# Batched matmul, 32 x (512x1024 by 1024x768): stores 0 to 10 move from the even to the odd turns of the load loop

## The chip, the cores and the metric

The kernel runs on one core of one Trainium2 chip. The metric is device time in microseconds (us), the median of several executions; smaller is better. The core has a matrix engine (TensorE, PE in the profile), three engines for copies and element work (VectorE or DVE, ScalarE or ACT, GpSimd or POOL), a synchronising engine (SyncE or SP), and 16 DMA engines that move data between the device's memory (HBM) and the core's own memory (SBUF). PE writes its results to a small accumulator memory (PSUM). DMAs are issued by an engine's instruction stream and then run from a queue: POOL feeds the software queue q0, SP the hardware queue q1.

## The reference

```python
batch, m, k, n = 32, 512, 1024, 768
x = np.random.randn(batch, m, k).astype(np.float32)
weight = np.random.randn(batch, k, n).astype(np.float32)

def reference(x, weight):
    return np.matmul(x, weight).astype(np.float32)
```

There are 32 independent products. Each reads 2 MiB of x and 3 MiB of weight and writes 1.5 MiB of result, all float32 in HBM. The whole problem reads 167.77 MB and writes 50.33 MB.

## The kernel before

**Tiling.** Two batch entries form a pair, so there are 16 pairs, 0 to 15. The x of a pair is one DMA of 4 MiB on the HBM side, the weights of a pair are one DMA of 6 MiB (called w(k) here for pair k; the first two pairs and the last one are loaded as two DMAs of one entry each), and a finished pair's results are one store of 3 MiB. x and w become bf16 on the way into SBUF. The page of the profile gives the bytes of such a load on the SBUF side, half of those read.

**Buffers.** There are two x slots, two pairs' worth of w slots and four output slots (`W_SLOTS, X_SLOTS, OUT_SLOTS = 4, 2, 4`, the first counted in entries). Output slot a % 4 can be written again when the store of pair a - 4 has landed: `slot_free` (line 231) makes ACT wait for that before its first copy of a pair, and lets DVE go on through the semaphore `s_free`.

**PE** (`on_pe`, from line 192) goes through the pairs in order. For each pair it transposes x in 8 groups (line 174, result tile `pt`, spread by DVE into `xT` at line 220, or 228 for the last pair), and then multiplies: 2 entries x 4 row tiles, each 16 matmuls on lines 139 and 166 into the six accumulator tiles `pm`. It takes a ready signal for the pair's x ahead of the transposes and one for each entry's w ahead of that entry's matmuls.

**ACT and DVE** copy the accumulators into the output slots (lines 262 and 266 on ACT, 271 and 273 on DVE). The copy at line 273 is the last one of half an entry. DVE does the last copy of pair k only after it has spread the transposes of pair k + 1.

**POOL** (`on_pool`) issues nearly all the DMAs, in the program's order, and waits in that order too. The loop is written out for 14 turns, k = 0 to 13. Turn k issues x(k + 2), when the first row tile of pair k has been multiplied (`mm_begun(k)`, line 110); then, in some turns, stores; then w(k + 2), when pair k has been multiplied completely (line 97; the two entries of pair 15 have a wait each, line 101). A store (`store`, line 117) first waits until ACT and DVE have copied the whole pair. Behind the loop POOL issues stores 11, 12 and 13. q0 works these DMAs off in the order of issue.

**SP** waits for each load of w and passes the signal on to PE, and then issues the last output itself: store 14, and the output of pair 15 in four quarters (lines 119 and 124) as its entries' halves are copied.

The diff touches one condition in `on_pool`; the loop counts `PAIRS = 16`, `HELD = 2`.

Of the kernel before, what the change touches and what calls it, by code (L numbers as in the profile page):

```python
# [12 lines left out]
def kernel(  # L13
# [16 lines left out]
    PAIRS = B // 2  # L30
# [62 lines left out]
    def load_w(b):  # L93
        if together(b):
            if b % 2 == 0:
                pool.wait_ge(s_mm, mm_done(b + 1 - W_SLOTS))
                slots = all_ws[:, b // 2 % 2].rearrange("p r ko n -> p r (ko n)")
                pool.dma_start(out=slots, in_=w_two_view[b // 2]).then_inc(s_w[b % W_SLOTS], 16)  # L98
            return
        if b >= W_SLOTS:  # L100
            pool.wait_ge(s_mm, mm_done(b - W_SLOTS))
        pool.dma_start(out=ws[b % W_SLOTS], in_=w_view[b]).then_inc(s_w[b % W_SLOTS], 16)  # L102
# [5 lines left out]
    def load_x(k):  # L108
        if k >= X_SLOTS:
            pool.wait_ge(s_mm, mm_begun(k - X_SLOTS))  # L110
        pool.dma_start(out=xs[k % X_SLOTS], in_=x_view[k]).then_inc(s_x[k % X_SLOTS], 16)  # L111
# [5 lines left out]
    def store(eng, a, sem):  # L117
        copied(eng, 4 * a + 3)
        eng.dma_start(out=two_view[a], in_=outs[a % OUT_SLOTS]).then_inc(sem, 16)  # L119
# [222 lines left out]
    def on_pool():  # L342
        load_w(0)
        pool.memset(ident, 0.0).then_inc(s_zero, 1)  # L344
        pool.wait_ge(s_zero, 1)
        pool.affine_select(  # L346
            out=ident,
            in_=ident,
            compare_op=mybir.AluOpType.not_equal,
            fill=1.0,  # L350
            base=0,
            pattern=[[-1, P]],
            channel_multiplier=1,
        ).then_inc(s_ident, 1)
        load_w(1)
        load_x(1)
        load_w(2)
        load_w(3)
        def stores(first, last):
            for a in range(max(first, 0), last):  # L360
                store(pool, a, s_st[a % OUT_SLOTS])


        for k in range(PAIRS - 2):
            load_x(k + 2)
            if k % 2 == 0:
                stores(k - 3, k - 1)
            load_w(2 * k + 4)
            load_w(2 * k + 5)
        stores(PAIRS - 3 - HELD, PAIRS - 2)  # L370
# [21 lines left out]
    with tc.tile_critical(sync_engine=mybir.EngineType.Activation, no_gpsimd_drain=True):  # L392
        sp.dma_start(x_first, x_view[0]).then_inc(s_first, 16)
        on_pool()
        on_pe()
        on_dve()
        on_act()
        on_sp()
        clear_on_pool()
# [30 lines left out]
```

## Time and profile before

| what | before |
|---|---|
| median of 3 runs | 512.89 us (512.43 to 513.11) |
| span of the profiled execution, first to last instruction | 510.1 us |
| median minus that span (what lies around it) | 2.8 us |
| PE busy | 422.5 us, 83% |
| DVE busy | 212.8 us, 42% |
| ACT busy | 115.8 us, 23% |
| POOL busy | 29.0 us, 6% |
| mean granted PE clock | 0.951 |

The profile is of one execution, and gives no time for it beside the span. A row of a timeline or a group reads: start, duration (or busy time and mean), engine, line of the kernel, operation, tiles, count, and in square brackets the idle time of that engine ahead of it with what ended it. DMA-issuing instructions last about half a microsecond; how long the data takes stands in the DMA views, as the time from the issue to the landing of the last byte. In the rows of time stretches, the number behind PEclk's place is the granted TensorE clock, then come the mean busy share of the 16 DMA engines (it can come out a little over 1, since packets overlap) and the rate, which counts a load by its bf16 bytes.

### The profile page before, as it was taken

The numbers are of one execution on the slowest core, as the hardware profiler recorded it, in microseconds if no ns is written. First come the engines' busy times: TensorE is split into PE (matmuls) and PEld (weight loads), VectorE is DVE, ScalarE is ACT, GpSimd is POOL, SyncE is SP. The second block draws the span as 40 slices with busy tenths as digits, with TensorE's granted clock in tenths as the row PEclk, the third lists the DMA queues.
The fourth block names the chain that finished last, engine by engine and source line by source line (L and its number), as shares of the span: only waits on it lengthen the run. The fifth ranks groups of instructions, "written<-read, shape, count | busy, mean of one in ns | idle before, by whom it ended". The sixth has DMA issues, their size and how long they took to land. (4 is left out here: it accounts for less than half of the span.)

```text
span 510.1 us, 5783 instructions
## 1 busy us (share of the span) xinstructions
PE 422.5 (83%) x2512; PEld 172.3 (34%) x1536; DVE 212.8 (42%) x332; ACT 115.8 (23%) x197; POOL 29.0 (6%) x54
## 2 busy tenths in 40 slices
PE   0199999999999599993999939999499984999990
PEld 0143425353525134251343403434144331343420
DVE  0253636454536136351463513635145441454631
ACT  1313131313231221302313023130222302223130
POOL 2000001000100001000010000100001000100000
PEclk9999999999999899997999969999799995999996
DMA  8999999999999999999999999999999999999997
GB/s 296 261 213 216 217 215 220 212 299 251 214 217 224 432 241 218 215 229 432 233 219 216 244 432 216 220 216 259 419 216 218 219 272 405 215 215 236 434 427 336
DMA packets 9443, 136.34 MB, mean 267 GB/s; under 512 B 864, under 2 KB 864, under 8 KB 1376
## 3 DMA queue, kind: packets, MB, share of 16 engines
q0 software_dynamic: 8576, 125.83, 95.7%
q1 hardware_dynamic: 864, 10.49, 5.0%
q14 instruction: 3, 0.02, 0.0%
HBM read 167.77 MB, written 50.33 MB: 428 GB/s over the span
## 5 line engine op out<-in xcount | busy, mean ns | idle before, releaser
L166 PE MATMUL pm<-w,xT 128*128 x976 | 328.2, 386 | 36.3 <-DVE outs L271 36.3
L139 PE MATMUL pm<-w,xT 128*128 x1024 | 283.9, 277 | 4.7 <-DVE xT L220 1.7
L166 PEld LDWEIGHTS pm<-w,xT 128*128 128x128 bf16 x1024 | 101.8, 99 | 275.4 <-issue 235.8
L271 DVE COPY outs<-pm 64x512 f32<-64x512 f32 x128 | 88.1, 688 | 199.8 <-DVEq L269 198.4
L262 ACT COPY outs<-pm 64x512 f32<-64x512 f32 x128 | 74.1, 579 | 264.1 <-PE pm L139 163.2
L174 PE MATMUL pt<-ident,x 128*128 128x128 f32 x512 | 84.5, 307 | 33.4 <-PEq L178 23.1
L220 DVE COPY xT<-pt 128x1024 bf16<-128x1024 bf16 x120 | 77.8, 687 | 63.4 <-PE pt L174 63.0
L174 PEld LDWEIGHTS pt<-ident,x 128*128 128x128 f32 x512 | 71.2, 210 | 48.7 <-issue 26.5
L266 ACT COPY outs<-pm 64x512 f32<-64x512 f32 x64 | 37.0, 578 | 99.9 <-PE pm L139 99.8
L273 DVE COPY outs<-pm 64x512 f32<-64x512 f32 x64 | 43.9, 685 | 0.0
L98 POOL DMA_DIRECT2D w<-in_weight_dram x13 | 9.2, 706 | 260.0 <-PE pm L139 260.0
L111 POOL DMA_DIRECT2D x<-in_x_dram x15 | 8.3, 555 | 127.3 <-PE pm L139 88.7
L281 DVE CAST x<-outs 128x1024 bf16<-128x1024 f32 x4 | 2.5, 690 | 18.9 <-DMA outs<-in_x_dram 18.9
L119 POOL DMA_DIRECT2D out_dram<-outs x14 | 7.5, 537 | 7.1 <-DVE outs L273 7.1
L281 ACT CAST x<-outs 128x1024 bf16<-128x1024 f32 x4 | 3.9, 1042 | 16.6 <-DMA outs<-in_x_dram 16.6
L228 DVE COPY xT<-pt 128x512 bf16<-128x512 bf16 x16 | 5.7, 418 | 4.1 <-PE pt L174 4.1
L102 POOL DMA_DIRECT2D w<-in_weight_dram x6 | 3.4, 564 | 29.1 <-PE pm L139 27.9
L281 ACT ACT_TABLE_LOAD x1 | 1.3, 1283 | 1.0 <-ACTq L392 1.0
L346 POOL TENSOR_SCALAR_AFFINE_SELECT ident<-ident 128x128 f32<-128x128 f32 x1 | 0.3, 282 | 0.2 <-POOL ident L344 0.2
L344 POOL MEMSET ident<- 128x128 f32 x1 | 0.2, 223 | 0.0
L414 POOL MEMSET const-float32-0.0<- 128x1 f32 x1 | 0.1, 98 | 0.2 <-issue 0.2
L414 POOL MEMSET const-bfloat16-1.0<- 128x1 bf16 x1 | 0.1, 102 | 0.0
(2 smaller groups left out, 0.2 us busy)
## 6 DMA issues: line engine op xcount, KB each, us to landing
out_dram<-outs POOLq DMA_DIRECT2D x14, 3072.0 KB, 39.0
w<-in_weight_dram POOLq DMA_DIRECT2D x13, 3072.0 KB, 29.1
x<-in_x_dram POOLq DMA_DIRECT2D x15, 2048.0 KB, 30.4
w<-in_weight_dram POOLq DMA_DIRECT2D x6, 1536.0 KB, 29.8
outs<-in_x_dram SPq DMA_DIRECT2D x1, 4096.0 KB, 18.0
out_dram<-outs SPq DMA_DIRECT2D x1, 3072.0 KB, 18.8
out_dram<-outs SPq DMA_DIRECT2D x4, 768.0 KB, 15.2
```

The costliest lines, as they stand in the source:

```text
L98: pool.dma_start(out=slots, in_=w_two_view[b // 2]).then_inc(s_w[b % W_SLOTS], 16)
L111: pool.dma_start(out=xs[k % X_SLOTS], in_=x_view[k]).then_inc(s_x[k % X_SLOTS], 16)
L119: eng.dma_start(out=two_view[a], in_=outs[a % OUT_SLOTS]).then_inc(sem, 16)
L139: return pe.add_instruction(mybir.InstMatmult(name=nc.get_next_instruction_name(), engine=mybir.EngineType.PE, ins=[pe.lower_ap(moving), p ...
L166: last = pe.matmul(*args, start=(ko == 0), stop=(ko == KT - 1))
L174: last = pe.transpose(pts[g % 2][:, j, :], words[:, mo, j::JT], ident)
L220: return dve.tensor_copy(both[g // 2][:, :, :, g % 2].rearrange("p b j i r -> p j b i r"), pt)
L262: last = act.copy(*piece)
L266: act.copy(*pieces(b, p, 2)[0]).then_inc(s_ap, 1)
L271: last = dve.tensor_copy(*piece)
L273: dve.tensor_copy(*pieces(b, p, 2)[1]).then_inc(s_dp, 1)
L281: last = copy(xs[0][:, mo], x_first[:, mo])
```

## The change

```diff
         for k in range(PAIRS - 2):
             load_x(k + 2)
-            if k % 2 == 0:
-                stores(k - 3, k - 1)
+            if k % 2 and k < PAIRS - 3:
+                stores(k - 2, k)
             load_w(2 * k + 4)
             load_w(2 * k + 5)
         stores(PAIRS - 3 - HELD, PAIRS - 2)
```

`stores(first, last)` issues stores first to last - 1, leaving out negative numbers. Before, store 0 stands in turn 2, and the couples (1, 2), (3, 4), (5, 6), (7, 8) and (9, 10) in turns 4, 6, 8, 10 and 12, always between that turn's x and its w. After, store 0 stands in turn 1 and the couples in turns 3, 5, 7, 9 and 11; turn 13 has none. So each of these 11 stores is issued one turn earlier, and the younger store of turn k is that of pair k - 1 instead of k - 2. In q0, store 0 passes w(3) and x(4), stores 1 and 2 pass w(5) and x(6), and so on up to stores 9 and 10, which pass w(13) and x(14): before, the order is x(14), store 9, store 10, w(14), x(15), w(15); after, it is x(13), store 9, store 10, w(13), x(14), w(14), x(15), w(15). The stores behind the loop and SP's stores keep their places, and the number and size of all DMAs are unchanged.

## The prediction

> **What bounds the kernel now.** I read the page first, for the bytes and the DMA queues, then rates by time stretch, then the list of waits, and last the timelines of POOL, PE and SP around pairs 13 to 15, since the end is made there. The page:
>
> ```profile
> span 510.1 us, 5783 instructions
> q0 software_dynamic: 8576, 125.83, 95.7%
> q1 hardware_dynamic: 864, 10.49, 5.0%
> HBM read 167.77 MB, written 50.33 MB: 428 GB/s over the span
> ```
>
> The two queues together keep the 16 DMA engines busy for 100.7% of the span (packets overlap a little). The stretches from 6 us to 508 us, and from there to the end, say the same:
>
> ```profile
> 6.00:508.00 502.00, 422.45 (x2512) 172.30 (x1536) 212.85 (x332) 114.55 (x196) 25.48 (x43) 0.95 1.01 268
> 508.00:510.10 2.10, 0.00 (x0) 0.00 (x0) 0.00 (x0) 0.00 (x0) 0.00 (x0) 0.50 0.02 9
> ```
>
> DMA share 1.01 over 502 us, and 0.02 after 508. So data moves without a break until 508.05 or so. The times to landing give the price of each kind of transfer. These are the DMAs issued in turn 12 and x(15) of turn 13; POOL's timeline has the issues, the DMA view of the same stretches the time to landing:
>
> ```profile
> 388.29 0.56 POOL L111 DMA_DIRECT2D x<-in_x_dram  x1 [7.72 <-DVE outs L273]
> 388.85 1.06 POOL L119 DMA_DIRECT2D out_dram<-outs  x2
> 406.49 0.71 POOL L98 DMA_DIRECT2D w<-in_weight_dram  x1 [16.58 <-PE pm L139]
> 414.77 0.56 POOL L111 DMA_DIRECT2D x<-in_x_dram  x1 [7.58 <-PE pm L139]
> ```
> ```profile
> out_dram<-outs POOLq DMA_DIRECT2D x1, 3072.0 KB, 37.1
> x<-in_x_dram POOLq DMA_DIRECT2D x1, 2048.0 KB, 30.4
> ...
> w<-in_weight_dram POOLq DMA_DIRECT2D x1, 3072.0 KB, 41.2
> ...
> x<-in_x_dram POOLq DMA_DIRECT2D x1, 2048.0 KB, 42.6
> ```
>
> Landings: x(14) at 388.3 + 30.4 = 418.7, store 9 at 388.85 + 37.1 = 426.0, w(14) at 406.5 + 41.2 = 447.7, x(15) at 414.8 + 42.6 = 457.4. Differences: a store takes 7.3 us of the queue, an x 457.4 - 447.7 = 9.7, a w 447.7 - 426.0 - 7.3 (store 10) = 14.4. In HBM bytes (3.15, 4.19 and 6.29 MB) each is 430 to 437 GB/s, so a store costs the same wherever it stands. All 218.1 MB at 432 GB/s are 505 us. **The kernel is bound by the bytes, and by nothing else in the middle.**
>
> PE is not the bound, but it waits for this queue:
>
> ```profile
> ACT outs L262 <- DMA out_dram<-outs: 100.2, 6, 19.2
> PE pm L166 <- DVE outs L271: 36.3, 5, 8.2
> ```
> ```profile
> 426.06 1.17 ACT L262 COPY outs<-pm 64x512 f32<-64x512 f32 x2 [19.18 <-DMA out_dram<-outs]
> ```
> ```profile
> 427.80 0.59 PE L166 MATMUL pm<-w,xT 128*128 x1 [8.13 <-DVE outs L271]
> ```
>
> ACT may not write pair 13 into its slot before store 9 has landed (426.0); ACT's row starts there, DVE follows, and PE stands still for 8.13 us until 427.80. Five odd pairs, 5 to 13, do this: that is what the change acts on.
>
> **The change part by part.** *The stores themselves.* Eleven stores move, none is added. Their issue costs POOL about 0.53 us each in either place, beside idle times of 7.6 to 16.6 us. Price 0.
>
> *The wait ahead of the store.* In turn k the younger store is now that of pair k - 1, whose last copy is DVE's, line 273:
>
> ```profile
> 387.31 0.69 DVE L273 COPY outs<-pm 64x512 f32<-64x512 f32 x1
> ```
>
> In turn 12 the last copy of pair 11 ends at 388.00, while POOL reaches the stores at 388.85, because x(14) ahead of them waits for pair 12's first row tile. A store of pair k - 1 is thus ready by 0.85 us, and by more where PE starts pair k late. What is queued behind it on POOL is w(k + 2), which waits 16.58 us for the end of pair k anyway; nobody waits for POOL meanwhile. Price 0; without that cover, a few tenths of queue slack, not of time.
>
> *The slot wait goes.* In q0 the order becomes x(13), store 9, store 10, w(13): both stores land ahead of the weights that pair 13 needs, so slots for pairs 13 and 14 are free before PE can start. All five stalls for stores vanish.
>
> *What is late next: w of the odd pairs.* w(13) is now followed only by x(14) and w(14) before 447.7, the bytes up to there being the same. So w(13) lands at 447.7 - 14.4 - 9.7 = 423.6; before, it stood ahead of x(14), store 9, store 10 and w(14), at 409. The same holds two turns apart for w(5) to w(11), each period of x, two stores, w, x, w being 2 x 9.7 + 2 x 7.3 + 2 x 14.4 = 62.8 us. PE needs less than that for two pairs, here the groups that start pair 14's matmuls, pair 15's transposes, pair 15's matmuls, and the last one:
>
> ```profile
> 449.34 0.27 PE L139 MATMUL pm<-w,xT 128*128 x1 [0.20 <-DVE xT L220]
> ...
> 469.93 1.13 PE L174 MATMUL pt<-ident,x 128*128 128x128 f32 x8
> ...
> 476.08 0.27 PE L139 MATMUL pm<-w,xT 128*128 x1
> ...
> 496.56 0.27 PE L139 MATMUL pm<-w,xT 128*128 x1
> ```
>
> Matmuls of a pair take 469.93 - 449.34 = 20.6 us, transposes 476.08 - 469.93 = 6.15. Two pairs are 53.5 us, plus a slow restart (below), so PE stands at each odd pair for about 62.8 - 53.5 - 2 = 7 us: as long as before, but waiting for w. Since each odd pair starts afresh with its w, nothing adds up from pair to pair.
>
> *The clock after the wait.* The stretches of the stall, the restart and what follows:
>
> ```profile
> 419.70:427.80 8.10, 0.00 (x0) 0.03 (x1) 1.52 (x3) 1.70 (x4) 0.00 (x0) 0.68 1.00 431
> 427.80:432.90 5.10, 4.87 (x16) 1.25 (x9) 0.46 (x1) 1.10 (x3) 0.00 (x0) 0.50 0.99 388
> 432.90:443.40 10.50, 10.45 (x65) 3.23 (x33) 3.96 (x6) 3.47 (x6) 0.53 (x1) 1.00 1.03 219
> ```
>
> After the idle time PE ran 5.1 us at clock 0.50, a loss of 2.55 us. Pair 7's restart:
>
> ```profile
> 238.80:241.70 2.90, 2.68 (x8) 0.65 (x5) 0.43 (x1) 1.06 (x3) 0.00 (x0) 0.50 1.02 441
> ```
>
> There only 2.9 us ran at half clock, a loss of 1.5 us. I take 2.3 for the new stall, nearer the first, whose place it has. Bounds: 1.5, and 4.6, an estimate for a half clock that lasts 9.2 us, nearly twice the longer of the two rows. The Trainium skill (TensorE: Matmul & The Clock Gate, Part 1) says that a window of about 3.4 us, free-running, decides on half or full clock; by that rule the loss would be between half a window and a whole one, 1.7 to 3.4 us by my estimate, and the row agrees.
>
> *The end of PE's work.* Pair 13 starts at 423.6 + 0.2 for the signals through SP = 423.8. Then 20.6 + 2.3 (pair 13), 6.1 + 20.6 (pair 14), 6.15 + 20.75 (pair 15): 500.3, against 496.83 (the last row above). PE ends 3.5 us later, 2.7 to 5.8 with the bounds of the clock. No slot stops it: ACT's first copy of pair 15 waited for store 11 before,
>
> ```profile
> 479.44 1.17 ACT L262 COPY outs<-pm 64x512 f32<-64x512 f32 x2 [8.65 <-DMA out_dram<-outs]
> ```
>
> and that store keeps its place in q0, so it lands at about 479.3 again; ACT now wants it after pair 15's first row tile, 2.6 us behind 479.6.
>
> *What that does to the end.* SP's stores are the last bytes:
>
> ```profile
> L124 SPq DMA_DIRECT2D out_dram<-outs x4: 332/332/333, 483.5 to 499.1; - x4
> L119 SPq DMA_DIRECT2D out_dram<-outs x1: 342/342/342, 478.9 to 478.9; - x1
> ```
> ```profile
> out_dram<-outs SPq DMA_DIRECT2D x1, 768.0 KB, 10.1
> ```
>
> The last quarter is issued at 499.1 and lands 10.1 us later, though its 0.786 MB need only 7.3 / 4 = 1.83 us: it stands behind others. Its data starts at 508.05 - 1.83 = 506.2. Whatever delays its issue is free until the queue ahead of it would run out, at 506.2. How long an issue on q1 takes to move data is bounded by store 14, issued at 478.9, in these two stretches, 479 to 482.5 and 482.5 to 483.5:
>
> ```profile
> q0 software_dynamic: 61, 1.50, 99.5%
> ...
> q1 hardware_dynamic: 13, 0.32, 74.4%
> ```
>
> q1 moved nothing until 482.5: up to 3.6 us. The last quarter, issued at 499.1 + 3.5 = 502.6, would start by 506.2 even so. That is just in time, cost 0 to 0.1. At the far end, 499.1 + 5.8 + 3.6 = 508.5, cost 2.3 us. Below zero nothing can come of it: the bytes are fixed, and no stretch has idle DMA engines to fill. The Trainium skill (DMA: Bandwidth & Descriptors, Latency and other measured facts) gives about 0.6 us to the first byte for a queue like SP's; by it the sum would be 0 with 3 us in hand, and the row here differs, at up to 3.6 us beside a busy q0.
>
> *The head and the queue.* Would the queue run dry anywhere, since odd turns now issue later? x(15) would be issued about 3 us after 423.8 and w(14) at pair 12's end, about 410; their data starts at 447.7 and 433.2, so 20 us of queue stand ahead of either. In turn 1 store 0 comes behind x(3), and w(3) lands 7.3 us later, just ahead of pair 3. No price.
>
> **Sum.** Bytes 0, waits of POOL 0, PE's end +3.5 of which 3.5 are covered, end of the last store 0 to +0.1: span 510.2. The profiled execution's span is 510.1 and the median 512.89, so 2.8 us lie around it, which the change doesn't touch: 513.0 us. About 0.2% (1.0 us) is what a measurement of this kernel can tell from no change.
>
> **Rivals.**
>
> 1. *Slower: the last quarter comes too late.* One mechanism: PE, restarted at w(13), takes longer at half clock, and SP issues the last quarter when q1 has run out. It decides once PE's delay exceeds 3.5 us with the 3.6 us latency, and is beyond 0.2% from 4.5 us on; at 5.8 us it gives 512.9 + 2.3 = 515.2. For it: the cover is used up in my sum. Against: the 3.6 us were measured beside a full q0, which is almost empty at 503, and the next DMA of a queue need not wait for the one ahead.
>
> The last stretch before 508 us, for rival 2:
>
> ```profile
> 503.00:508.00 5.00, 0.00 (x0) 0.00 (x0) 0.00 (x0) 0.00 (x0) 0.00 (x0) 0.50 0.94 392
> ```
>
> 2. *Faster: the store stalls go and PE ends early.* Pair 13 would save 8.13 + 2.55 = 10.7 us, and if w(13) did not take the stall's place, PE would end at 486. The time would still be that of the bytes; only the last five microseconds, which moved 392 GB/s where 432 are usual, could close up, by 5 x 0.09 = 0.5 us: 512.4. The DMA share of 1.01 speaks against more.
>
> 3. *The change does not free the slots earlier in effect, because POOL stands at the store of pair k - 1.* Then q0 would be filled later. It needs a delay beyond the 16.6 us that POOL idles ahead of w, and then beyond 20 us of queue. Time: 512.9, as before.
>
> **How the numbers follow.** The forecast, no change that can be told, 513.0 us, gets 0.80 (rival 3, 0.03, ends in the same place: together 0.83). Rival 1 gets 0.13, rival 2 beyond 0.2% gets 0.04. So faster 0.04, same 0.83, slower 0.13. The range starts at 512.2, a little under the fastest run shown, and reaches to 514.6, most of the way to rival 1's end at 515.2.
>
> **What would show it.** Right: the wait of ACT for the output's DMAs falls from 100.2 us to almost nothing, PE's five waits for DVE's copies go, and five waits of 6 to 9 us ahead of the matmuls of pairs 5, 7, 9, 11 and 13 take their place; the DMA share stays at 1.01; PE ends at 499.5 to 502.5; the last quarter is issued at about 502.6 and lands about 6.5 us later instead of 10.1. Wrong: DMA engines idle anywhere from 6 us to 508 us, or a last quarter that lands as soon as its issue allows, with the span growing in step.

## The result and the profile after

The changed kernel takes 513.75 us (median of 6 runs, 513.53 to 514.49); the kernel before, run beside it, 512.23 us (511.87 to 513.11). The ratio is 1.0031, with a 95% interval of 1.0021 to 1.0042: slower by 0.31%, 1.5 us between the medians. The time lies in the forecast range, and 0.75 us above the value forecast, but the kernel before came out 0.7 us lower beside it than in the runs that the forecast started from. So the change cost 1.5 us where 0.1 was forecast, and "no change that can be told", which the forecast drew at 0.2%, did not hold.

The page of after, in the lines that the prediction shows of before:

```profile
span 512.3 us, 5831 instructions
...
q0 software_dynamic: 8576, 125.83, 95.3%
q1 hardware_dynamic: 864, 10.49, 4.9%
...
HBM read 167.77 MB, written 50.33 MB: 426 GB/s over the span
```

The same bytes in a span 2.2 us longer, and in the stretch from 6 to 508 us the DMA share (the last number but one) is what it was:

```profile
6.00:508.00 502.00, 427.84 (x2560) 172.93 (x1536) 212.93 (x332) 115.35 (x196) 25.56 (x43) 0.95 1.01 268
```

The list of waits of after:

```profile
PE pm L166 <- PEq L178: 40.5, 5, 9.6
```

The 100.2 us that ACT waited for stores and PE's five waits for DVE's copies are gone from it. In their place PE waits five times, 40.5 us in all, at line 178, which is where it takes the signals that loads have landed. So the stalls did change from a wait for the slot to a wait for w. POOL's issues of turn 11 and of x(14), PE's restart at pair 13, three stretches around it (the columns are again granted clock, DMA share and rate at the end of each row), and the time to landing of the w issued at 386.22:

```profile
367.99 0.56 POOL L111 DMA_DIRECT2D x<-in_x_dram  x1 [18.62 <-PE pm L139]
368.54 1.07 POOL L119 DMA_DIRECT2D out_dram<-outs  x2
386.22 0.71 POOL L98 DMA_DIRECT2D w<-in_weight_dram  x1 [16.61 <-PE pm L139]
394.70 0.56 POOL L111 DMA_DIRECT2D x<-in_x_dram  x1 [7.77 <-PE pm L139]
```
```profile
425.76 0.61 PE L166 MATMUL pm<-w,xT 128*128 x1 [7.48 <-PEq L178]
```
```profile
418.30:425.70 7.40, 0.00 (x0) 0.00 (x0) 2.69 (x5) 0.00 (x0) 0.00 (x0) 0.77 1.06 225
425.80:429.00 3.20, 3.20 (x11) 0.81 (x6) 0.00 (x0) 0.00 (x0) 0.00 (x0) 0.50 1.05 225
429.10:448.00 18.90, 18.90 (x118) 5.67 (x58) 5.95 (x9) 6.39 (x11) 1.09 (x2) 1.00 1.00 212
```
```profile
w<-in_weight_dram POOLq DMA_DIRECT2D x1, 3072.0 KB, 39.1
```

w(13) landed at 386.2 + 39.1 = 425.3, and PE restarted at 425.76 after 7.48 us. The forecast had 423.6 and 423.8. Two microseconds are lost already here, in the middle of the kernel. PE's last matmul and SP's stores in after:

```profile
501.43 0.27 PE L139 MATMUL pm<-w,xT 128*128 x1
```
```profile
L124 SPq DMA_DIRECT2D out_dram<-outs x4: 332/332/333, 488.4 to 504.0; - x4
L119 SPq DMA_DIRECT2D out_dram<-outs x1: 342/342/342, 483.8 to 483.8; - x1
```
```profile
out_dram<-outs SPq DMA_DIRECT2D x1, 768.0 KB, 7.4
```

PE ends 4.9 us later than before and the last quarter is issued at 504.0, so rival 1 looks likely at first. But look at what the DMA engines do at the very end. First before, then after:

```profile
506.00:508.00 2.00, 0.00 (x0) 0.00 (x0) 0.00 (x0) 0.00 (x0) 0.00 (x0) 0.50 0.83 347
508.00:508.50 0.50, 0.00 (x0) 0.00 (x0) 0.00 (x0) 0.00 (x0) 0.00 (x0) 0.50 0.06 25
508.50:510.00 1.50, 0.00 (x0) 0.00 (x0) 0.00 (x0) 0.00 (x0) 0.00 (x0) 0.50 0.01 4
```
```profile
506.00:508.00 2.00, 0.00 (x0) 0.00 (x0) 0.00 (x0) 0.00 (x0) 0.00 (x0) 0.50 0.86 359
508.00:508.50 0.50, 0.00 (x0) 0.00 (x0) 0.00 (x0) 0.00 (x0) 0.00 (x0) 0.50 0.06 25
508.50:510.00 1.50, 0.00 (x0) 0.00 (x0) 0.00 (x0) 0.00 (x0) 0.00 (x0) 0.50 0.07 29
510.00:511.00 1.00, 0.00 (x0) 0.00 (x0) 0.00 (x0) 0.00 (x0) 0.00 (x0) 0.50 0.04 18
```

A DMA share of 0.06 is one engine of sixteen (1/16 = 0.0625). In both kernels the bulk is done at 508. Before, one engine works on alone until 508.7 us, in after until 510.9 us; the spans differ by the same 2.2 us. In every profile of this case the span ends 1.2 to 1.6 us behind the last packet of data, so the engine that ends last sets the time. A last quarter that came too late would hold up all sixteen (a run below shows how that looks).

The trace also holds the landing signals: a DMA raises its semaphore by 16, once for each engine. For w(14), the last load of two entries, the first of the 16 signals comes at 447.0 us before and 446.9 us after, the last one 0.73 us behind it before and 2.65 us behind it after. The last but one comes 0.65 and 0.88 us behind the first. So one engine has fallen behind by 2 us, long before the end, while the other fifteen are nearly on time. The lag grows step by step: in after the distance from the first to the last signal is 0.65 us for the load of w that lands at 76 us, 0.99 at 195, 1.33 at 258, 1.68 at 321, 2.26 at 384 and 2.65 at 447; before, it stays between 0.6 and 0.8 us for all of these loads. PE has to wait for the slowest: the first signal of w(13) came at 422.7 us, the last, 2.65 us later, at 425.3.

### The profile page after: what moved, and what is told of

It is laid out like the page before. It is cut to its first block, busy times and chain, and to the rows that moved or that the text cites. A ratio compares the mean times of both kernels' runs of the same rounds, so it can differ in the third digit from the quotient of the medians.

```text
span 512.3 us, 5831 instructions
## 1 busy us (share of the span) xinstructions
PE 427.8 (84%) x2560; PEld 172.9 (34%) x1536; DVE 212.9 (42%) x332; ACT 116.6 (23%) x197; POOL 29.1 (6%) x54
## 5 line engine op out<-in xcount | busy, mean ns | idle before, releaser
L166 PE MATMUL pm<-w,xT 128*128 x1024 | 344.6, 388 | 40.7 <-PEq L178 40.5
L139 PE MATMUL pm<-w,xT 128*128 x1024 | 284.2, 278 | 0.0
```

The lines of the kernel that those rows point to most:

```text
L139: return pe.add_instruction(mybir.InstMatmult(name=nc.get_next_instruction_name(), engine=mybir.EngineType.PE, ins=[pe.lower_ap(moving), p ...
L166: last = pe.matmul(*args, start=(ko == 0), stop=(ko == KT - 1))
```

## The experiments

Two theories. A: one DMA engine loses time at stores that run beside busy engines; before, the slot wait kept PE still, or at half clock, during the stores, and the change took that away. B: PE's later end makes the last quarter late (rival 1).

**The change again, and its two halves.** The edits are shown as cuts of the code; `...` stands for lines left out. The first run is the changed kernel once more. The next two split it in the place where the theories differ: the order around pair 13 decides how late PE ends, the order of the eight stores ahead of it how many stores run beside a busy PE.

> The changed kernel once more, beside the runs that follow. Two theories stand for its +1.5 us (0.31%). Theory A, the slow DMA engine: in the profile of after, 15 of the 16 DMA engines are done at 508.1 us as before, and one alone works on to 510.9 us. It falls behind by about 0.2 us at each store that runs beside a busy PE; before, the slot wait kept PE still or at half clock while the stores ran. Theory B, the late end: PE ends 4.9 us later and SP's last quarter of the output, issued that much later, comes too late. Both expect +1.0 to +2.0 us here (ratio 1.002 to 1.004), and A that the DMA share of the last 2 us is again 0.06, which is one engine of sixteen.

Measured: 513.80 us, 1.0037 (1.0024 to 1.0051). Again one engine works on after 508:

```profile
508.00:508.50 0.50, 0.00 (x0) 0.00 (x0) 0.00 (x0) 0.00 (x0) 0.00 (x0) 0.50 0.06 25
508.50:510.00 1.50, 0.00 (x0) 0.00 (x0) 0.00 (x0) 0.00 (x0) 0.00 (x0) 0.50 0.07 29
```

```diff
-            if k % 2 == 0:
+            if k % 2 == 0 and k < PAIRS - 4:
                 stores(k - 3, k - 1)
+            if k == PAIRS - 5:
+                stores(k - 2, k)
```

> Only stores 9 and 10 move, from turn 12 to turn 11; stores 0 to 8 stay in the even turns. w(13) is then as late as in after, and PE ends as late (about 501.5 us), while only two of ten stores of the loop run beside a busy PE. Theory B (late end): +1.5 us, the whole loss of after. Theory A (slow DMA engine): a fifth of 2 us, +0.3 to +0.5 us, not to be told from no change.

Measured: 512.67 us, 1.0014 (1.0005 to 1.0023). PE ended at 500.9 us in the profiled execution, nearly as late as in after, for 0.7 us of time by the medians: half of what B wants, a little over A.

```diff
-            if k % 2 == 0:
-                stores(k - 3, k - 1)
+            if k % 2 and k < PAIRS - 5:
+                stores(k - 2, k)
+            if k == PAIRS - 4:
+                stores(k - 3, k - 1)
```

> Stores 0 to 8 move to the odd turns, stores 9 and 10 stay in turn 12, so pair 13 waits for store 9 as before and PE ends as before (about 497 us). Theory B (late end): 0 within 0.3 us. Theory A (slow DMA engine): eight of ten stores run beside a busy PE, +1.0 to +1.7 us, and one DMA engine ends about 2 us behind the others.

Measured: 513.22 us, 1.0027 (1.0016 to 1.0038). PE's last matmul and the end of this run:

```profile
496.59 0.27 PE L139 MATMUL pm<-w,xT 128*128 x1
```
```profile
506.00:508.00 2.00, 0.00 (x0) 0.00 (x0) 0.00 (x0) 0.00 (x0) 0.00 (x0) 0.50 0.70 292
508.00:508.50 0.50, 0.00 (x0) 0.00 (x0) 0.00 (x0) 0.00 (x0) 0.00 (x0) 0.50 0.06 25
508.50:510.00 1.50, 0.00 (x0) 0.00 (x0) 0.00 (x0) 0.00 (x0) 0.00 (x0) 0.50 0.06 25
```

PE ends at 496.9 us, as before, and yet 1.3 us are lost, with one engine working on alone. B falls here as the cause of the whole. The two halves add up: 0.14% + 0.27% against 0.31 and 0.37% for the whole.

**A late end alone.** The loop of before, with PE's end made late in another way:

```diff
             if k % 2 == 0:
                 stores(k - 3, k - 1)
+            if k == PAIRS - 3:
+                stores(k - 2, k)
...
-        stores(PAIRS - 3 - HELD, PAIRS - 2)
+        stores(PAIRS - 3, PAIRS - 2)
```

> The loop of before, but stores 11 and 12 stand ahead of the last pair's weights instead of behind them. The weights of pair 15 land 14.6 us later (479.3 and 486.6 us), so PE starts pair 15 about 3.4 us later and ends at 500 to 503 us, as late as in after; the stores of the loop run beside a stalled PE as before. Theory B (late end): +1.0 to +2.0 us. Theory A (slow DMA engine): 0 to +0.4 us.

Measured: 512.22 us, 1.0007 (0.9998 to 1.0016), with executions from 511.79 to 513.90. The profiled one is the slowest of them. In it PE ended at 504.3 us, 2.6 us later than in after; where PE ended in the others is not known. Its last quarter, issued at 506.5, landed 3.9 us later, and the end of this execution is another than that of after:

```profile
out_dram<-outs SPq DMA_DIRECT2D x1, 768.0 KB, 3.9
```
```profile
506.00:508.00 2.00, 0.00 (x0) 0.00 (x0) 0.46 (x1) 0.00 (x0) 0.00 (x0) 1.00 0.41 169
508.00:508.50 0.50, 0.00 (x0) 0.00 (x0) 0.00 (x0) 0.00 (x0) 0.00 (x0) 1.00 0.94 393
```

The DMA engines ran dry (share 0.41 from 506 to 508) and then all worked again (0.94). That is rival 1 as described: this execution took 2.0 us more than the median of before, at a later PE than the change makes. So a late end can cost time, and the median of this run doesn't refute B by itself. What it adds is the size of the cover. Fifteen engines, with nothing left ahead of the quarter, moved its first data 0.9 us after the issue and had it landed after 3.3 us; the 3.9 us are those of the slowest engine. In after the last quarter was issued at 504.0, so its data could have started at about 504.9, while the engines had other work until about 506 (508 less the 1.8 us of the quarter itself). It landed at 511.3, behind the slow engine's backlog. The cover was still there.

**PE kept busy in the order of before.** In pairs 5, 7, 9, 11 and 13, ahead of the wait, PE does 21 pairs of matmuls whose results nobody reads (`keep_busy`, into the transposes' accumulators):

```diff
+                    if b == 0 and mt == MT - 1:
+                        for k in range(5, PAIRS - 2, 2):
+                            with pe.If_eq(pair, k):
+                                keep_busy(w_pair[:, 0, 0])
                     at = 2 * b + mt // 2 + 1 + mt % 2
...
```

> The kernel before, with the order of its stores, but in pairs 5, 7, 9, 11 and 13 PE does about 7 us of matmuls into the transposes' accumulators, whose results nobody reads, just where it would stand waiting for a store. PE is then busy while the loop's stores run; ACT and DVE still wait for the slot. Theory A1 (one DMA engine is slowed by a store beside a busy PE): +1.0 to +2.0 us against before. Theory A2 (by a store beside copies of ACT and DVE into the output slots): 0 to +0.5 us. Theory B (late end) was for PE's end alone, which is not later here than before: 0.

Measured: 513.00 us, 1.0013 (1.0004 to 1.0022), a little under half of the loss, though the order of the DMAs is that of before and PE ends at 497.0. More work on PE, done where it would idle anyway, makes the kernel slower. That is between A1 and A2. Stores 9 and 10 in this run, and store 10 before:

```profile
417.40:424.70 7.30, 7.30 (x46) 2.15 (x22) 0.00 (x0) 0.00 (x0) 0.00 (x0) 1.00 0.98 421
424.70:432.10 7.40, 6.01 (x37) 1.76 (x18) 2.16 (x4) 3.06 (x6) 0.07 (x1) 1.00 1.01 417
```
```profile
425.20:432.80 7.60, 4.77 (x15) 1.26 (x9) 1.98 (x3) 2.80 (x5) 0.00 (x0) 0.50 1.00 407
```

Store 9 runs beside PE alone, store 10 beside PE at full clock and the copies of DVE and ACT (the third and fourth busy times); before, store 10 ran beside the same copies, but PE was at half clock. The table of packets below uses this.

**All stores on SP's queue.**

```diff
                 landed(sp, s_w[b % W_SLOTS], loads_of_w(b), s_wr, 1 + together(b))
+                now = {B - 2: (PAIRS - 5,), B - 1: (PAIRS - 4, PAIRS - 3)}.get(b, (b // 2 - 2,))
+                for a in now if 4 <= b < B - 6 and b % 2 == 0 or b >= B - 2 else ():
+                    store(sp, a, s_st[a % OUT_SLOTS])
```

and no stores on POOL.

> The changed kernel with all of stores 0 to 13 issued by SP on the hardware queue q1: one each behind the landing of the weights of pairs 2 to 12, store 11 behind the first weights of pair 15, stores 12 and 13 behind the second. They run beside a busy PE. If only stores of the software queue lose time on one DMA engine: one engine no longer ends late, 0 to -0.8 us against before, so 1 to 2 us under after. If any store beside a busy PE loses: +1 to +2 us against before, like after.

Measured: 512.43 us, 1.0006 (0.9997 to 1.0015). Here stores 0 to 10 alternate with the loads of q0, packet by packet, and no engine falls behind: the signals of w(14) lie 0.68 us apart. It doesn't beat the kernel before. But the words "of the software queue" in the expectation fall: stores 12 to 14, which have the DMA engines to themselves near the end, beside a PE that works until 500.6 us, show 7, 7 and 6 slow packets in q1 too (slow as defined in the table below). The Trainium skill (DMA: Bandwidth & Descriptors, Latency and other measured facts) says that two of the sixteen engines are usually slower, and gives as a best guess, specific to the software queue, contention at the ports by its descriptor rings; these packets of q1 speak against that as the only cause here. The trace doesn't say which engine it is.

**PE with less work.** Half, or seven eighths, of the sum over K are left out; all DMAs stay.

```diff
-        for ko in range(KT):
+        for ko in range(KT // 2):
...
```

> The changed kernel with half of the sum over K left out (the second four of eight steps of each product), so PE does 10 us of matmuls a pair instead of 20.6; all DMAs are the same. Theory A: PE stands still during most of each couple of stores, so the slow engine loses little; -1.0 to +0.4 us against before, and within 0.7 us of the next run. The end is not late in either.

Measured: 512.75 us, 1.0014 (1.0005 to 1.0023): +0.6 us, outside what was expected.

> The kernel before with the same half of the sum over K left out. Theory A: like the run of the changed order with half the work, within 0.7 us; -1.0 to +0.4 us against before. If the order of the stores in the queue itself cost the time, whatever PE does, the difference of 1.5 us would stay.

Measured: 511.60 us, 0.9993 (0.9984 to 1.0003). The difference between the two is 1.15 us, more than the 0.7 that theory A allowed. In the changed order the second store of each couple ran beside the transposes, with PE at a clock of 0.89 to 1.00, and DVE's copies of them, so the engines weren't idle there as I had assumed. In the order of before, the first store of a couple ran beside idle engines and the second beside PE at half clock and the copies:

```profile
417.60:424.90 7.30, 0.00 (x0) 0.00 (x0) 0.00 (x0) 0.00 (x0) 0.00 (x0) 0.55 1.00 431
424.90:432.50 7.60, 4.90 (x17) 1.23 (x9) 3.96 (x6) 3.38 (x6) 0.53 (x1) 0.53 0.99 407
```

With one eighth of the work:

```diff
-        for ko in range(KT):
+        for ko in range(1):
...
```

> The changed kernel with seven of the eight steps of the sum over K left out; PE does 2.6 us of matmuls a pair and stands still otherwise, beside 6 us of transposes; all DMAs and copies are the same. The second store of each couple then runs beside idle engines, the first beside transposes. Theory A: almost no packet of a second store above 930 ns, no engine more than 1 us behind at the end, -0.8 to +0.3 us against before. If the order in the queue costs the time without the engines: +1 to +2 us.

Measured: 512.39 us, 1.0005 (0.9995 to 1.0014), in the changed order. The end of this run:

```profile
506.00:508.00 2.00, 0.00 (x0) 0.00 (x0) 0.00 (x0) 0.00 (x0) 0.00 (x0) 0.50 0.79 329
508.00:508.50 0.50, 0.00 (x0) 0.00 (x0) 0.00 (x0) 0.00 (x0) 0.00 (x0) 0.50 0.03 12
508.50:510.00 1.50, 0.00 (x0) 0.00 (x0) 0.00 (x0) 0.00 (x0) 0.00 (x0) 0.50 0.00 0
```

No engine works on alone from 508.5 us. By its interval the order of the queue costs at most 0.14% by itself, not the 0.31% of the change; the order of before with one eighth of the work was not run beside it.

**Single stores.** One store in each turn instead of couples:

```diff
-            if k % 2 == 0:
-                stores(k - 3, k - 1)
+            if k < PAIRS - 3:
+                stores(k - 2, k - 1)
```

> One store in each of turns 2 to 12 (that of pair k - 2) between that turn's x and w, no couples; all by POOL as before. In the profiles so far the packets of one DMA engine take 20 to 60 ns longer than 912 ns when stores run beside busy engines: about 2 of a first store's packets, 7 or 8 of the second's that follows it directly, none where stores alternate with loads packet by packet. If the loss needs several microseconds of stores alone: each store is like a first one, 0.05 to 0.1 us each, +0.3 to +1.0 us against before, and 0.5 to 1.2 us less than after. If it only needs busy engines: +1.3 to +2.0 us, like after.

Measured: 513.77 us, 1.0033 (1.0020 to 1.0045), as slow as after. That the loss would need two stores in a row is refuted: every store now runs alone, beside PE at full clock and the copies, and the loss is there.

**Packets.** The trace has the duration of each DMA packet. A store is 128 packets of 24,576 bytes, 8 for each engine; they take 912 ns (925 directly after a load). In the changed kernel's second stores of a couple there are about 8 that take more, mostly by 20 to 60 ns, at most by 113: as many as one engine has. And they are those of one engine. Nearly every packet of a couple starts within 4 ns of the end of another, so the 256 packets can be linked into 16 chains of 16, one for each engine. In after, all slow packets of a couple stand in one chain in four of the five couples (11, 9, 9 and 9 packets); for stores 7 and 8 the links are not clear. For stores 1 to 10 in the profiled execution of each kernel (slow means over 930 ns; the third column is their sum over 912 ns; the last the distance from the first to the last landing signal of w(14)):

```
kernel              slow, store 1 to 10          sum    w(14)    ratio
before              0 2 0 2 0 1 0 2 1 1   =  9   0.4 us  0.73 us  1
after               4 7 2 7 2 7 3 9 1 8   = 50   1.8     2.65     1.0031
after again         3 7 2 6 3 6 2 8 2 8   = 47   1.6     2.12     1.0037
only 9 and 10       0 3 0 2 0 0 0 3 3 7   = 18   0.6     1.28     1.0014
all but 9 and 10    2 8 4 6 2 7 3 8 0 6   = 46   1.6     2.09     1.0027
late end            0 4 0 2 0 0 0 3 1 1   = 11   0.3     1.79     1.0007
PE kept busy        0 7 1 7 0 6 0 6 1 7   = 35   1.2     2.39     1.0013
after, half K       3 6 3 5 1 7 2 5 1 6   = 39   1.4     2.40     1.0014
before, half K      0 0 0 0 0 0 0 0 0 0   =  0   0       0.80     0.9993
one store a turn    3 2 3 2 4 4 4 4 3 4   = 33   1.2     2.80     1.0033
after, one eighth   1 2 1 1 1 2 2 1 1 2   = 14   0.6     0.95     1.0005
```

The sum for after, 1.8 us, is nearly the 1.9 us by which w(14) is further apart than before. The split halves show slow packets just in the stores that moved. In the run with PE kept busy the first store of a couple stays clean although PE is busy (ACT and DVE wait for the slot during it), while the second, beside matmuls at full clock and the copies, is nearly as slow as in after; in the order of before that second store ran beside the copies and PE at half clock, and had 1 or 2 slow packets. So neither matmuls alone nor the copies with PE at half clock do it; the two together, at full clock, do, and with half K the transposes and their copies do it as well. Which shared resource it is stays open, and whether recording the profile has a part in it too. The single profiles also hold other delays: the late-end run has before's order in the loop, few slow packets, and still 1.79 us at w(14), and in the run with PE kept busy 1.2 of the 2.39 us were there before the first store. With one store a turn the slow packets sum to 1.2 us only, for a ratio like that of after. So the columns agree with the ratios only roughly.

## What the prediction had right and wrong

That the time fell into the forecast range is in part luck: the forecast started from a median 0.7 us above the one measured beside the change. It also added 2.8 us for what lies around the span, from a median and a span that need not be of the same execution; in the six executions of after this is 2.1 us. Without these 0.7 us the same sum would have given 512.3, and the loss of 1.5 us would stand out. Such a loss had no place in the working.

The waits were right. The stores were ready without a wait; ACT's waits for stores went; five waits of 7.1 to 9.6 us for w took the place of the slot waits; the half clock after the restart lasted 3.2 us at pair 13, a loss of 1.6 us, just inside the bounds; the DMA share stayed at 1.01 over 502 us; the queue never ran dry in the middle.

The step that failed is in the first part of the working: "so a store costs the same wherever it stands", and with it "Price 0" for the stores themselves. It was read from stores 9 and 10, which ran beside a halted or slowed PE: the cadence of 7.3 us is theirs, and I carried it over to stores beside a busy one. There each costs one engine about 0.2 us, 1.8 us for ten, and a transfer, and the kernel, ends with its slowest engine. The profile before had such stores too: stores 0, 11, 12 and 13 ran beside PE at full clock there, and have 3, 4, 5 and 5 slow packets. The forecast named a DMA share that stays at 1.01 among its signs of being right. It stayed; a mean over sixteen engines doesn't show the sixteenth that arrives late.

PE's end was forecast at 500.3 us and measured at 501.7: 2 us came from the late landing of w(13), and the half clock gave 0.7 us back. The cover at the end was forecast to be just used up, with 3.6 us from the issue of the last quarter to its data. That was measured beside a full q0; with the queues nearly empty, in the late-end run, it was 0.9 us, so the cover was larger.

Rival 1 had the right sign and a price of the right order, but it was not what made the loss: with PE's end as before the ratio was still 1.0027, and in the profile of after one engine alone is late, not all sixteen. Whether a late end adds some tenths in other executions is not shown. Of the signs said to show the forecast wrong, the span grew, but neither idle DMA engines ahead of 508 us (the share is 1.01) nor a last quarter that lands as soon as its issue allows were there. The case that came was on no list.

## What to carry to other kernels

A kernel whose DMA engines are all busy still ends with the slowest of them: read the tail in short stretches, and take a share of 1/16 as one engine that lags. Filling another engine's idle time need not be free in such a kernel: here that idle time was what let the stores beside it run at full pace. When a transfer is moved, its duration must be read from a place with the same neighbours as its new one.

## What was unexpected of the hardware

Store packets of one DMA engine took mostly 20 to 60 ns longer than 912 ns beside PE at full clock and busy copies, and none did where PE, with half of the work left out, ran at half clock or stood still (before, half K: 0 of 1,280). Where stores alternated with loads packet by packet, stores 0 to 10 had no slow packet either, but seven of every eight packets of each engine took 925 ns: 13 ns x 7 packets, about 0.1 us for each store on every engine. Over 11 stores that is an estimated 1 us, which may be why that version doesn't gain.
